# Overflow loads on GpSimd's queue, the next layer's rows loaded early, a second gather round moved back, and the last norm's Newton steps on GpSimd, in a two-layer decoder trunk

## The chip, the cores and the metric

The kernel runs on one core of a Trainium2 chip. TensorE (PE in the views; PEld is its weight load) multiplies matrices into PSUM, VectorE (DVE) and ScalarE (ACT) do element-wise work, GpSimd (POOL) a little of it, and SyncE (SP) issues the loads and stores, which 16 DMA engines carry out. An issuing engine works through its instructions in order, so an issue that waits holds all issues behind it on that engine. The metric is device time in microseconds (us).

## The reference

Two layers run on x of 256 tokens by 1024 channels. Each has a token mixer (four branches read one input projection; their outputs are gated, merged and projected) and a mixture of 16 experts in 4 groups, of which every token uses 2 of one group. Behind each sublayer stands a layer norm of 2^0.5 times the input plus the sublayer's output:

```
for l in range(DEPTH):
    mix = token_mixer(x, ...)                                 # w_in, four branches, w_branch, w_o
    x = layer_norm(DEEPNORM_ALPHA * x + mix, ln1_g, ln1_b)
    ffn = hierarchical_moe(x, ...)                            # router, experts of hidden width 256
    x = layer_norm(DEEPNORM_ALPHA * x + ffn, ln2_g, ln2_b)
```

An expert is `silu(x @ w_gate) * (x @ w_up)`, weighted by the router's gate and multiplied with `w_down`. Everything is float32.

## The kernel before, in words

**Weights.** The weights lie in DRAM as units of 128 x 2048 floats, 1 MB each. `Unit` (line 111) loads one with an issue of SP (line 117). A mixer unit is then split: ACT copies it into a rounded high part (line 134), DVE subtracts that from the original into a low part (line 138), and TensorE multiplies high and low parts (`three`, line 229). An expert's three units (gate and up for half of the channels, for the other half, and down) are used unsplit. Their buffers are a ring of 14 (4 of tag `raw`, 10 of tag `sp`, shown as raw and wr); `look(n)` issues units ahead, each as soon as the unit 14 places before it has been used.

**Experts.** The tokens of an expert are gathered by a matmul with a one-hot matrix Q into 64 slots. Two experts make a pair. Six pairs are worked off, with pair numbers 0 to 5, and the last "pair", number 6, holds the four smallest experts with 32 slots each. From expert 6 on, the order is by token count and the unit's address is read from a tile (`unit_of`). `pair(p)` does on TensorE: gate and up of pair p + 1 (`gu`, line 699), transposes (lines 738 and 740), the scatter of pair p - 1 into the four sums `acc` (line 715), the second half of gate and up, and pair p's down projection (`out_`, line 707). ACT and DVE split its result into two parts `yy` (lines 96 and 97). The gathers come in two rounds: the first for pairs 0 to 2, the second in `pair(1)`, eight channel blocks of four matmuls (line 533). Each block goes to one of two PSUM banks of tag `dn` and is evacuated by ACT (line 539) or DVE (line 541), which read gain and bias of the first norm from the rows tile `rw`. The down projection uses the same two banks.

**Overflow.** An expert with more than 64 tokens needs more slots. If the largest one has more, a branch (line 797) issues its three units on SP into `ow` and `od` (`fetch`, line 691), and a second branch (line 852) runs `chunk` with them, interleaved with the last two down projections. A branch in between (line 807, `rare`) holds the loads and the work of further overflowing experts. In the execution shown layer 0 has no overflow, layer 1 has one expert with it, and `rare` is passed over in both.

**Order.** Blocks under `manual()` run on TensorE, ACT and DVE as written; elsewhere, and on SP and GpSimd everywhere, a planner sets the order from its own estimates. Layer l's `rw` and `bc` (gains, biases, small weights) are loaded at the start of `layer` (line 1095), into one buffer each. At the end of a layer's experts come `out6`, `scatter6`, `turn7` and `down7` for the last two pairs, and `ahead(0)` to `ahead(5)`: the splits of the next layer's first three units. The last result is then split (`parts_of` into y7) and scattered, and 14 matmuls without use (`keep_warm`) follow in layer 0.

**Last norm.** `Norm` takes mean and variance, makes a first guess of the inverse root and a halved variance `hv` (line 278), and `newton` improves it three times with two operations of one element per partition (lines 283 and 284). `scale` (line 295) subtracts the mean from the sums in PSUM and multiplies by the gain; `shift` (line 298) multiplies by the root and adds the bias. `norm2` puts the three Newton steps between the scalings.

Of the kernel before, what the change touches and what calls it, by code (L numbers as in the profile page):

```python
# [19 lines left out]
L = 2  # L20
# [49 lines left out]
def trunk(ctx: ExitStack, tc: tile.TileContext, x, xT, wu, rows, brow, lnp, cst, ut, out):  # L70
# [195 lines left out]
    class Norm:  # L266


        def __init__(self, st, mv=None):
            t_ = lambda s_, w=1: sm.tile([P, w], F32, tag="ln" + s_, name=nm("n" + s_))  # L270
            self.mv = mv
            if mv is None:
                self.mv = t_("mv", 2)
                V.bn_aggr(self.mv, st)
            self.v, self.y, self.hv, self.nmu, self.a = t_("v"), t_("y"), t_("hv"), t_("nmu"), t_("a")
            V.tensor_scalar(self.v, self.mv[:, 1:2], EPS, None, op0=OP.add)
            V.tensor_scalar(self.y.bitcast(I32), self.v.bitcast(I32), -0.5, 1597463007.0, op0=OP.mult, op1=OP.add)
            V.tensor_scalar(self.hv, self.v, -0.5, None, op0=OP.mult)
            if mv is None:
                V.tensor_scalar(self.nmu, self.mv[:, 0:1], -1.0, None, op0=OP.mult)  # L280
# [5 lines left out]
        def all(self):  # L286
            for _ in range(3):
                self.newton()

        def offset(self):  # L290
# [125 lines left out]

    def tail(l, x_in, mhi, mlo, rw, wg, sw, unit, last):

# [117 lines left out]
        def gathered(c, k):  # L536
            g_, b_ = rw[:, W_G1 + k:W_G1 + k + 1], rw[:, W_B1 + k:W_B1 + k + 1]
            if k % 2 == 0:
                A.activation(xg[c][:, k, :], pgs[k], AF.Identity, bias=b_, scale=g_)
            else:  # L540
                V.tensor_scalar(xg[c][:, k, :], pgs[k], g_, b_, op0=OP.mult, op1=OP.add)  # L541

        look(8)
        def keep_warm(q, n, ps):
# [4 lines left out]
        with manual():  # L549
# [88 lines left out]

            def unit_of(i, j):
                eu = nc.values_load(ei[0:1, i:i + 1], engines=(mybir.EngineType.SP,), min_val=l * NU + FIRST_E,  # L640
                                    max_val=l * NU + FIRST_E + 45)
                return wu[bass.ds(eu + j, 1)].rearrange("a p c -> p (a c)")
# [48 lines left out]
            def fetch(i, ww, wd):  # L691
                for j, w in enumerate((ww[:, 0:2048], ww[:, 2048:4096], wd)):
                    nc.sync.dma_start(w, unit_of(i, j))

# [75 lines left out]
            def pair(p, si, todo, ps=None):  # L770
                ps = ps or start(p + 1)
                qt, aT = turn(p, si)
                if todo:
                    scatter(*todo)
                si = end(p + 1, ps)
                for k in more.get(p, ()):
                    for t in range(2):
                        gather(1, k, t)
                    gathered(1, k)
                if p == 1:  # L780
                    slot_gates(STAT // 2, NP)
                return si, out_(p, qt, aT)

# [52 lines left out]
        def scatter6(half):  # L836
            scatter(*todo, (half,), (0,))
# [14 lines left out]
        with tc.If(most > 16 * CAP + 15, label=f"past{l}") as c:  # L852
            with manual():
                steps.chunk(0, CAP, (lambda: out6(0), lambda: out6(1), lambda: scatter6(0),
                                     lambda: (scatter6(1), turn7()), lambda: (ahead(0), down7((0,)))))
                ahead(1)
                down7((1,))
        with c.Else(), manual():
            out6(0)
            out6(1)  # L860
            scatter6(0)
            scatter6(1)
            turn7()
            ahead(0)
            ahead(1)
            down7()
        with manual():
            if last:
                A.activation(gs[:, 0:1], gs[:, 0:1], AF.Square)
            ahead(2)  # L870
            y = mp.tile([P, 2, D], F32, tag="T16a", name=nm("y"))
            y7 = big.tile([P, 2, 2, 512], F32R, tag="xtok", name=nm("y7"))
            yy = [parts_of((ps, tp6)[half], y7[:, half]) for half in range(2)]

            scatter(NP - 1, qt7, yy, (0, 1), (0,))
# [24 lines left out]
            def norm2(t):  # L900
                n_ = Norm(st[t])
                n_.newton()
                for half in range(2):
                    scale(n_, t, half)
                    n_.newton()
                for half in range(2):
                    last_ = shift(n_, t, half)
                return last_
# [3 lines left out]
            if last:  # L912
# [3 lines left out]
                for half in range(2):  # L916
                    A.activation(y[:, 1, HS[half]], acc[1][half], AF.Identity, accum_out=sq[:, half:half + 1])
                n0 = Norm(st[0])
                n0.newton()
                scale(n0, 0, 0)  # L920
                n0.newton()
# [5 lines left out]
                n0.newton()  # L927
                shift(n0, 0, 0)
# [3 lines left out]
                V.tensor_scalar(mv[:, 1:2], sq[:, 2:3], sq[:, 3:4], 1.0 / D, op0=OP.add, op1=OP.mult)  # L932
                n1 = Norm(None, mv)
                n1.newton()
                scale(n1, 1, 0)
                n1.newton()
                scale(n1, 1, 1)
                n1.newton()
                for half in range(2):
                    shift(n1, 1, half)  # L940
                    done(1, half)
            else:
# [11 lines left out]
                nc.sync.dma_start(x2d, y)  # L954
        return None if last else (x2d, nhi, nlo, us[len(feed):])

# [117 lines left out]

    def layer(l, x_in, thi, tlo, last, early):

# [14 lines left out]
        us = [unit() for _ in range(2)]  # L1091
        rw = big.tile([P, W_N], F32, tag="rw", name=nm("rw"))
        bc = big.tile([P, B_N], F32, tag="bc", name=nm("bc"))
        with tc.issue_after(early[2].load.ins) if l == 0 else nullcontext():
            nc.sync.dma_start(rw, rows[l])
            nc.sync.dma_start(bc, brow[l].partition_broadcast(P))

# [265 lines left out]

        return tail(l, x_in, mhi, mlo, rw, wg, sw, unit, last)

    xt, (thi, tlo) = x, first
    for l in range(L):
        r = layer(l, xt, thi, tlo, l == L - 1, early)
        if r is not None:
            xt, thi, tlo, early = r  # L1370

# [110 lines left out]
```

## Time and profile before

| | |
|---|---|
| median of 3 runs | 689.94 us (687.84 to 691.34) |
| profiled execution | 687.56 us, span 685.8 us, mean granted clock 0.986 |
| PE busy | 652.8 us (95%) |
| PEld busy | 462.3 us (67%) |
| DVE busy | 412.3 us (60%) |
| ACT busy | 287.0 us (42%) |
| POOL busy | 5.9 us (1%), 26 instructions |
| DMA | 185.73 MB, mean 271 GB/s, all on one queue |
| raw and wr units from SP | 91 and 63 of 1024 KB, landing 5.2 and 9.5 us (median) after the issue |
| rows (rw) and brow (bc) | 2 of 478 KB and 2 of 458 KB |

The span is the time on the core; some 1.7 us of the device time lie around it. Busy shares are means over stages: in the experts the DMA engines are at times fully busy, in the mixers they are not. The chain of work that ended last goes back only to 647.87 us, so what set the time earlier is read from the timelines and the waits.

### The profile page before, as it was taken

How to read it: one execution, taken by the hardware profiler on the slowest of the kernel's cores; microseconds unless marked ns; L12 is line 12 of the kernel's file. 1: busy time of each engine (PE TensorE's matmuls, PEld its weight loads, DVE VectorE, ACT ScalarE, POOL GpSimd, SP SyncE). 2: the span in 40 equal slices, each digit the busy share in tenths (PEclk: the TensorE clock that was granted, in tenths of full speed). 3: DMA queues.
4: the chain of work that ended last, by engine and by line, in shares of the span. 5: the costliest groups of instructions: out<-in, count | busy, mean ns of one | idle time of the engine just before them, and what ended most of it. 6: DMA issues, size and time to landing. Idle time of an engine off the chain costs nothing. (4 is left out here: it accounts for less than half of the span.)

```text
span 685.8 us, 9776 instructions
## 1 busy us (share of the span) xinstructions
PE 652.8 (95%) x3579; PEld 462.3 (67%) x3579; DVE 412.3 (60%) x932; ACT 287.0 (42%) x465; POOL 5.9 (1%) x26
## 2 busy tenths in 40 slices
PE   8999999999999999998699999999999999999983
PEld 5899778888888354333479987888887953543331
DVE  4998667876557832211799875786853677321116
ACT  5755675454224231111455547664441252211122
POOL 0100000000000000000000000000000000000000
PEclk9999999999999999999899999999999999999997
DMA  8995544466759997979927363456566799699871
GB/s 302 369 338 190 206 131 176 172 219 224 289 192 391 410 419 290 396 291 424 421 100 275 123 236 105 152 183 249 182 225 265 271 409 421 261 402 418 318 326 62
DMA packets 28001, 185.73 MB, mean 271 GB/s; under 512 B 3104, under 2 KB 3232, under 8 KB 6432
## 3 DMA queue, kind: packets, MB, share of 16 engines
q1 hardware_dynamic: 27936, 184.94, 70.4%
q8 instruction: 32, 0.52, 0.3%
q14 instruction: 33, 0.27, 0.1%
HBM read 182.83 MB, written 2.10 MB: 270 GB/s over the span
## 5 line engine op out<-in xcount | busy, mean ns | idle before, releaser
L138 DVE TENSOR_TENSOR sp<-raw,sp 128x1024 fp32r<-128x1024 f32 x122 | 147.9, 1221 | 53.7 <-ACT sp L134 43.6
L134 ACT CAST sp<-raw 128x1024 fp32r<-128x1024 f32 x122 | 126.0, 1051 | 105.3 <-PE mm L229 72.5
L229 PE MATMUL mm<-sp,thi 128*128 128x512 f32 (+1 forms) x320 | 96.5, 382 | 1.5 <-ACT sp L96 0.9
L229 PE MATMUL mm<-sp,nhi 128*128 128x512 f32 (+1 forms) x320 | 97.4, 382 | 0.3 <-ACT nhi L96 0.3
L699 PE MATMUL ps<-wr,xg 128*64 128x512 f32 (+1 forms) x352 | 80.0, 596 | 0.0
L229 PEld LDWEIGHTS mm<-sp,thi 128*128 128x128 f32 x320 | 58.9, 188 | 13.5 <-ACT sp L96 1.5
L229 PEld LDWEIGHTS mm<-sp,nhi 128*128 128x128 f32 x320 | 58.8, 188 | 11.7 <-issue 0.5
L229 PE MATMUL mm<-sp,nlo 128*128 128x512 f32 (+1 forms) x160 | 61.4, 385 | 0.5 <-DVE nlo L97 0.4
L229 PE MATMUL mm<-sp,tlo 128*128 128x512 f32 (+1 forms) x160 | 60.1, 380 | 0.0
L699 PEld LDWEIGHTS ps<-wr,xg 128*64 128x64 f32 (+1 forms) x352 | 23.0, 128 | 37.2 <-issue 36.5
L229 PE MATMUL dn<-sp,yhl 128*128 128x512 f32 x192 | 47.8, 392 | 0.0
L409 DVE SCALAR_TENSOR_TENSOR si<-ps,gs,si 128x256 f32<-128x256 f32 x14 | 6.8, 483 | 62.6 <-ACT si L408 62.4
L699 PE MATMUL ps<-raw,xg 128*64 128x512 f32 (+1 forms) x144 | 43.2, 596 | 0.8 <-DVE xg L541 0.8
L229 PE MATMUL mm<-sp,mhl 128*128 128x512 f32 (+1 forms) x192 | 41.0, 368 | 0.9 <-ACT mhl L96 0.5
L229 PEld LDWEIGHTS dn<-sp,yhl 128*128 128x128 f32 x192 | 35.8, 188 | 7.4
L229 PEld LDWEIGHTS mm<-sp,mhl 128*128 128x128 f32 x192 | 32.6, 189 | 7.5 <-DVE mhl L97 1.1
L229 PE MATMUL mm<-thi,sp 128*128 128x256 f32 x192 | 35.6, 286 | 1.4 <-ACT scr L1225 1.3
L229 PE MATMUL mm<-nhi,sp 128*128 128x256 f32 x192 | 35.7, 286 | 0.3 <-ACT misc L1122 0.3
L97 DVE TENSOR_TENSOR yy<-dn,yy 128x512 fp32r<-128x512 f32 x24 | 16.4, 690 | 31.8 <-ACT yy L96 31.8
L229 PEld LDWEIGHTS mm<-sp,nlo 128*128 128x128 f32 x160 | 30.1, 188 | 6.6 <-DVE nlo L97 1.0
L229 PEld LDWEIGHTS mm<-sp,tlo 128*128 128x128 f32 x160 | 30.1, 188 | 5.5
L707 PE MATMUL dn<-wr,aT 128*64 128x512 f32 x112 | 31.5, 613 | 2.2 <-DMA wr<-in_wu_dram 2.2
(305 smaller groups left out, 974.8 us busy)
## 6 DMA issues: line engine op xcount, KB each, us to landing
raw<-in_wu_dram SPq DMA_DIRECT2D x91, 1024.0 KB, 5.2
wr<-in_wu_dram SPq DMA_DIRECT2D x63, 1024.0 KB, 9.5
w<-in_wu_dram SPq DMA_DIRECT2D x6, 1024.0 KB, 14.9
raw<-in_wu_dram SPq DMA_DIRECT2D x8, 256.0 KB, 6.0
lnp<-in_lnp_dram SPq DMA_DIRECT2D x4, 512.0 KB, 6.0
lnp<-in_lnp_dram SPq DMA_DIRECT2D x2, 1024.0 KB, 15.7
ow<-in_wu_dram SPq DMA_DIRECT2D x2, 1024.0 KB, 10.6
xr<-in_xT_dram SPq DMA_DIRECT2D x4, 256.0 KB, 5.8
```

The costliest lines, as they stand in the source:

```text
L97: eng.tensor_tensor(lo, src, f32(hi), op=OP.subtract)
L134: A.copy(self.parts[q][0], self.raw[:, q * 1024:(q + 1) * 1024])
L138: V.tensor_tensor(lo, self.raw[:, q * 1024:(q + 1) * 1024], f32(hi), op=OP.subtract)
L229: T.matmul(ps, a, b, start=(first and i == 0), stop=(last and i == n - 1))
L409: V.scalar_tensor_tensor(si, ps[:, 256:512], gate, si, op0=OP.mult, op1=OP.mult)
L699: T.matmul(ps[r, :], x_[:, 4 * kh + k, c], w_[:, k * 512:(k + 1) * 512], start=(kh == 0 and k == 0), stop=(kh == 1 and k == 3))
L707: T.matmul(pd[half][r, :], aT[:, k, r], w_[:, k * 1024 + half * 512:k * 1024 + (half + 1) * 512], start=(k == 0), stop=(k == 1))
```

## The change

- `fetch` issues its three loads on GpSimd's queue instead of SP's, in the branch at line 797 and in `rare`; the addresses are read on GpSimd.
- Gains and biases of the first norm (16 columns of `rw`) are copied into a tile `gb` of their own at the start of a layer, and the gathers' evacuations read that. Rows and brow of the next layer are issued in the tail of this one, between the sixth and the seventh expert unit.
- In `pair`, the down projection stands ahead of the second gather round.
- `down7` runs in one piece in the overflow's branch, ahead of its last scatter, and the last split (`parts_of` into y7) stands ahead of `ahead(1)` and `ahead(2)`.
- In the second norm all Newton steps run on GpSimd, as six `tensor_scalar` operations, beside the scalings; the negated mean is no longer made there.

```diff
+        def aside(self):
+            for _ in range(3):
+                G.tensor_scalar(self.a, self.y, self.hv[:, 0:1], self.y[:, 0:1], op0=OP.mult, op1=OP.mult)
+                G.tensor_scalar(self.y, self.a, 1.5, self.y[:, 0:1], op0=OP.add, op1=OP.mult)
...
+    def load_rows(l):
+        rw = big.tile([P, W_N], F32, tag="rw", name=nm("rw"))
+        bc = big.tile([P, B_N], F32, tag="bc", name=nm("bc"))
+        nc.sync.dma_start(rw, rows[l])
+        nc.sync.dma_start(bc, brow[l].partition_broadcast(P))
+        return rw, bc
...
-            g_, b_ = rw[:, W_G1 + k:W_G1 + k + 1], rw[:, W_B1 + k:W_B1 + k + 1]
+            g_, b_ = gb[:, k:k + 1], gb[:, KD + k:KD + k + 1]
...
+        look(6)
+        nxt = None if last else load_rows(l + 1)
         look(8)
...
-                    nc.sync.dma_start(w, unit_of(i, j))
+                    G.dma_start(w, unit_of(i, j, mybir.EngineType.Pool))
...
                 si = end(p + 1, ps)
+                todo = out_(p, qt, aT)
                 for k in more.get(p, ()):
                     for t in range(2):
                         gather(1, k, t)
                     gathered(1, k)
                 if p == 1:
                     slot_gates(STAT // 2, NP)
-                return si, out_(p, qt, aT)
+                return si, todo
...
-                                     lambda: (scatter6(1), turn7()), lambda: (ahead(0), down7((0,)))))
-                ahead(1)
-                down7((1,))
+                                     lambda: (scatter6(1), turn7()), lambda: (ahead(0), down7())))
...
             ahead(0)
-            ahead(1)
             down7()
...
-            ahead(2)
             y = mp.tile([P, 2, D], F32, tag="T16a", name=nm("y"))
             y7 = big.tile([P, 2, 2, 512], F32R, tag="xtok", name=nm("y7"))
             yy = [parts_of((ps, tp6)[half], y7[:, half]) for half in range(2)]
+            ahead(1)
+            ahead(2)
...
             def norm2(t):
-                n_ = Norm(st[t])
-                n_.newton()
+                n_ = Norm(st[t], offset=False)
+                n_.aside()
                 for half in range(2):
                     scale(n_, t, half)
-                    n_.newton()
...
+        gb = sm.tile([P, 2 * KD], F32, tag="gb", name=nm("gb"))
+        V.tensor_copy(gb, rw[:, W_G1:W_G1 + 2 * KD])
```

The norms of the last layer's end are changed in the same way as `norm2`.

## Rows read from the trace of the kernel before

**Rows 1.** The page's first part: busy us (share of span), instructions.
```profile
PE 652.8 (95%) x3579; PEld 462.3 (67%) x3579; DVE 412.3 (60%) x932; ACT 287.0 (42%) x465; POOL 5.9 (1%) x26
```

**Rows 2.** Stretches: length, busy by engine (instructions), granted clock, DMA share, GB/s.
```profile
257.50:265.00 7.50, 7.50 (x40) 3.27 (x40) 3.95 (x12) 1.71 (x3) 0.64 (x1) 1.00 0.45 120
302.50:310.00 7.50, 7.50 (x52) 3.43 (x48) 1.06 (x2) 1.24 (x3) 0.00 (x0) 1.00 0.37 142
592.50:600.00 7.50, 7.50 (x40) 3.37 (x40) 3.14 (x9) 1.80 (x3) 0.00 (x0) 1.00 0.25 62
645.00:650.00 5.00, 5.00 (x52) 1.67 (x51) 0.48 (x1) 0.43 (x2) 0.00 (x0) 1.00 0.38 93
329.40:336.20 6.80, 3.76 (x8) 2.70 (x9) 6.10 (x11) 4.26 (x6) 0.00 (x0) 0.50 1.02 423
```

**Rows 3.** What SP waited for, whole run: total us, times, longest us.
```profile
SPq L807 <- SPq L807: 31.2, 10, 5.6
...
SPq L117 <- PE dn L707: 23.7, 7, 11.8
...
SPq L1095 <- DVE xg L541: 8.2, 1, 8.2
```

**Rows 4.** Line 807 on SP, layers 0 and 1: durations ns, first and last start.
```profile
L807 SPq EVENT_SEMAPHORE  x9: 17/17/17, 299.3 to 306.4; - x9
...
L807 SPq EVENT_SEMAPHORE  x9: 17/17/17, 633.9 to 647.8; - x9
```

**Rows 5.** TensorE's timeline: start us, us, what, count [idle before, releaser].
```profile
322.77 0.62 PE L707 MATMUL ps<-raw,aT 128*32 128x512 f32 x1 [1.34 <-DMA raw<-in_wu_dram]
...
331.86 0.79 PE L715 MATMUL mm<-y,QT 128*128 128x512 f32 x1 [5.47 <-ACT y L96]
...
653.08 3.18 PE L707 MATMUL dn<-wr,aT 128*64 128x512 f32 x6 [2.19 <-DMA wr<-in_wu_dram]
...
658.60 1.94 PE L707 MATMUL dn<-wr,aT 128*64 128x512 f32 x8
```

**Rows 6.** ACT's timeline at the end of layer 0.
```profile
327.76 1.99 ACT L134 CAST sp<-raw 128x1024 fp32r<-128x1024 f32 x2 [7.17 <-issue]
330.28 1.04 ACT L134 CAST sp<-wr 128x1024 fp32r<-128x1024 f32 x1 [0.52 <-DMA wr<-in_wu_dram]
331.23 1.07 ACT L96 CAST y<-ps 128x512 fp32r<-128x512 f32 x2
```

**Rows 7.** DVE's timeline at the end of layer 0.
```profile
328.84 2.36 DVE L138 TENSOR_TENSOR sp<-raw,sp 128x1024 fp32r<-128x1024 f32 x2 [9.92 <-DMA wr<-in_wu_dram]
...
332.50 1.28 DVE L97 TENSOR_TENSOR y<-ps,y 128x512 fp32r<-128x512 f32 x2
...
338.75 1.41 DVE L298 SCALAR_TENSOR_TENSOR y<-y,ny,lnp 128x512 f32<-128x512 f32 x2
```

**Rows 8.** GpSimd's timeline: a memset, a cast, a select.
```profile
0.32 0.10 POOL L1471 MEMSET const-float32-0.0<- 128x1 f32 x1 [0.32 <-issue]
...
17.68 1.17 POOL L198 CAST identb<-cs 128x128 bf16<-128x128 f32 x1 [15.93 <-DMA cs<-in_cst_dram]
...
20.12 0.63 POOL L1164 TENSOR_SCALAR_AFFINE_SELECT rw<-rw 128x512 f32<-128x512 f32 x1
```

**Rows 9.** DVE's timeline beside these casts.
```profile
17.47 2.46 DVE L138 TENSOR_TENSOR sp<-raw,sp 128x1024 fp32r<-128x1024 f32 x2 [2.24 <-ACT sp L134]
```

**Rows 10.** DVE's timeline at the end of layer 1.
```profile
671.31 0.69 DVE L97 TENSOR_TENSOR y<-ps,y 128x512 fp32r<-128x512 f32 x1 [1.19 <-ACT y L96]
...
678.56 0.14 DVE L278 TENSOR_SCALAR nhv<-nv 128x1 f32<-128x1 f32 x1
...
679.07 0.74 DVE L295 SCALAR_TENSOR_TENSOR y<-mm,sq,lnp 128x512 f32<-128x512 f32 x1
...
681.16 1.41 DVE L298 SCALAR_TENSOR_TENSOR y<-y,ny,lnp 128x512 f32<-128x512 f32 x2
```

**Rows 11.** Line 533 in layer 0's second round: durations ns, first and last start.
```profile
L533 PE MATMUL dn<-Q,xh x16: 389/396/500, 249.8 to 257.6; 128*128 128x512 f32 x16
```

More of the change, by code (lines that the diff above doesn't have):

```diff
@@ L266, in trunk, with __init__ @@
     class Norm:
-        def __init__(self, st, mv=None):
+        def __init__(self, st, mv=None, offset=True):
             t_ = lambda s_, w=1: sm.tile([P, w], F32, tag="ln" + s_, name=nm("n" + s_))
@@ L278, in __init__ @@
             V.tensor_scalar(self.hv, self.v, -0.5, None, op0=OP.mult)
-            if mv is None:
+            if offset:
                 V.tensor_scalar(self.nmu, self.mv[:, 0:1], -1.0, None, op0=OP.mult)
@@ L415, in parts_of, with tail @@
         return yy
-    def tail(l, x_in, mhi, mlo, rw, wg, sw, unit, last):
+    def load_rows(l):
[4 more added lines that the diff above has]
+        return rw, bc
+    def tail(l, x_in, mhi, mlo, gb, wg, sw, unit, last):
         tks = [slice(0, P), slice(P, 2 * P)]
@@ L637, in counts, with unit_of @@
                 V.tensor_scalar(ei, ei, -3, 45 + l * NU + FIRST_E, op0=OP.mult, op1=OP.add)
-            def unit_of(i, j):
-                eu = nc.values_load(ei[0:1, i:i + 1], engines=(mybir.EngineType.SP,), min_val=l * NU + FIRST_E,
+            def unit_of(i, j, engine=mybir.EngineType.SP):
+                eu = nc.values_load(ei[0:1, i:i + 1], engines=(engine,), min_val=l * NU + FIRST_E,
                                     max_val=l * NU + FIRST_E + 45)
@@ L917, in tail @@
                     A.activation(y[:, 1, HS[half]], acc[1][half], AF.Identity, accum_out=sq[:, half:half + 1])
-                n0 = Norm(st[0])
-                n0.newton()
+                n0 = Norm(st[0], offset=False)
+                n0.aside()
                 scale(n0, 0, 0)
-                n0.newton()
                 scale(n0, 0, 1)
@@ L926, in tail @@
                     A.activation(y[:, 1, HS[half]], acc[1][half], AF.Square, bias=nmu, accum_out=sq[:, 2 + half:3 + half])
-                n0.newton()
                 shift(n0, 0, 0)
@@ L932, in tail @@
                 V.tensor_scalar(mv[:, 1:2], sq[:, 2:3], sq[:, 3:4], 1.0 / D, op0=OP.add, op1=OP.mult)
-                n1 = Norm(None, mv)
-                n1.newton()
+                n1 = Norm(None, mv, offset=False)
+                n1.aside()
                 scale(n1, 1, 0)
-                n1.newton()
                 scale(n1, 1, 1)
-                n1.newton()
                 for half in range(2):
@@ L954, in tail @@
                 nc.sync.dma_start(x2d, y)
-        return None if last else (x2d, nhi, nlo, us[len(feed):])
+        return None if last else (x2d, nhi, nlo, us[len(feed):], nxt)
     def overflow(topi, counts, spare, fetch, ww, wd, oo, q, gt, x1, sums):
@@ L1073, in overflow, with layer @@
         return SimpleNamespace(chunk=chunk, rare=rare, room=room)
-    def layer(l, x_in, thi, tlo, last, early):
+    def layer(l, x_in, thi, tlo, last, early, rwbc):
         nxt_u = [0]
@@ L1091, in layer @@
         us = [unit() for _ in range(2)]
[L1092 to L1096, printed above, removed]
+        if l == 0:
+            with tc.issue_after(early[2].load.ins):
+                rwbc = load_rows(0)
+        rw, bc = rwbc
+        gb = sm.tile([P, 2 * KD], F32, tag="gb", name=nm("gb"))
+        V.tensor_copy(gb, rw[:, W_G1:W_G1 + 2 * KD])
         misc = big.tile([P, 2048], F32, tag="xtok", name=nm("misc"))
@@ L1362, in layer @@
                 split(tp.rearrange("p (k c) -> p k c", k=4), mhi[d], mlo[d])
-        return tail(l, x_in, mhi, mlo, rw, wg, sw, unit, last)
-    xt, (thi, tlo) = x, first
+        return tail(l, x_in, mhi, mlo, gb, wg, sw, unit, last)
+    xt, (thi, tlo), rwbc = x, first, None
     for l in range(L):
-        r = layer(l, xt, thi, tlo, l == L - 1, early)
+        r = layer(l, xt, thi, tlo, l == L - 1, early, rwbc)
         if r is not None:
-            xt, thi, tlo, early = r
+            xt, thi, tlo, early, rwbc = r
 def constants():
```

## The prediction

> **What bounds the kernel now.** I read the page's busy line first. TensorE is busy 652.8 of 685.8 us and GpSimd 5.9 us in 26 instructions [rows 1]: little is to be won unless TensorE's gaps close, and GpSimd has room. Next, TensorE's timeline at the two places where it stands still for long. At the end of layer 0's experts it waits 1.34 us for a weight and then 5.47 us for ACT's copy of the last expert result, so it idles from 326.39 to 331.86. At the last experts of layer 1 it waits 2.19 us for a weight, and the six matmuls behind take 3.18 us where eight take 1.94 [rows 5]. Third, the table of stretches. After the first idle time the granted clock is 0.50 (1.2 GHz, the lower level) over 6.8 us. The same table shows the DMA engines standing still in four earlier stretches although weights are wanted later: of 7.5, 7.5, 7.5 and 5 us they are busy 0.45, 0.37, 0.25 and 0.38. That is 4.1, 4.7, 5.6 and 3.1 us without transfer, while TensorE is fully busy [rows 2]. Fourth, what SP waited for. The first stretch: 8.2 us at line 1095, the load of the next layer's rows, held until line 541 has read the old rows. The third: 11.8 us (the longest of its seven) until pair 1's down projection (line 707) frees a buffer [rows 3]. The second and fourth lie under SP's stay at line 807, the branch of the rare overflow: nine waits from 299.3 to 306.4 and from 633.9 to 647.8 [rows 4]. 1 MB at 423 GB/s [rows 2] is 2.5 us; nine waits over 13.9 us fit loads landing one after the other. I read them as SP emptying its queue because the branch holds loads of SP. So the late weights come from SP's order, not from too little bandwidth.
>
> **The change part by part.**
>
> *Overflow fetch on GpSimd.* With no load of SP in that branch, the nine waits go, and SP issues the next weights as buffers come free. Each fetch takes its offsets and three issues to GpSimd; behind it stand a few memsets and the last norm, far later. The 3 MB are the same 7.4 us at 423 GB/s on whichever queue. They would start when their buffers are free, in the stretch 592.5 to 600 that has 5.6 us to spare [rows 2], and are read only after 658.60 [rows 5]. No row shows a load issued by GpSimd; up to the 58 us between 600 and 658 it costs nothing, beyond that its excess. I take nothing.
> By the Trainium skill (DMA: Bandwidth & Descriptors, "Issuing engines are not separate DMA queues") a second issuing engine saves only issue time. By that rule this edit gains nothing by itself; the rows of line 807 show a cost that is order and not bandwidth. It is the third case below.
>
> *Rows early.* The copy of 16 columns into gb frees the rows' buffer early, so the load needs no line 541, and SP's 8.2 us go. rows and brow (0.94 MB, 2.2 us) leave this stretch for the token mixer. The copy is one small DVE operation per layer, like those of 0.14 us [rows 10], in a stretch where DVE is not the bound: nothing.
>
> *Second round reordered.* Pair 1's down projection goes ahead of the eight gathers, which run from 249.8 to about 258 [rows 11]. Its weight buffers are free some 8 us earlier, so SP's 11.8 us shrink to about 3. The price is in PSUM: the gathers use the same two banks as the down projection. The second bank is free after a copy and a subtraction of a half (0.54 and 0.69 us from the last parts [rows 6, 10], with handing over 1.4 us), the first gather lasts 1.0 us, and the second waits about 0.5 us. With two layers +1.0 us; bounds 0 and +2.8 (both halves uncovered).
>
> *Layer 0's end.* Before, ACT does two weight copies (327.76, 1.99 us), waits for a further weight (330.28) and only then copies the result (331.23) [rows 6]. Now one copy stands ahead. 4.1 + 4.7 us of DMA standstill are filled, so the first weight is there about 319 to 320, not 327.76, and is copied before the matmuls end. TensorE loses its 1.34 us wait and ends at 325.05. The second half is copied at 325.1 to 325.65 and subtracted to 326.4. What is late next: DVE now has two weight subtractions (2.36 us) ahead of the statistics. Before, from the end of the last subtraction (332.50 + 1.28 = 333.78) to the first shift (338.75) went 4.97 us [rows 7]. Now the shift starts at 326.4 + 2.36 + 4.97 = 333.7, less 0.3 for the norm below: 333.4. With the low clock gone from the scatter it may be 0.4 us less. I take 333.2: -5.5 us. Bounds: -1.8 (weights land no earlier: the copy at 328.8, the shift near 337) and -7.9 (the two subtractions cost nothing).
>
> *Layer 1's last experts.* The weight that TensorE waits for until 653.08 lands 5.3 us after SP's last wait at line 807 (647.8), two loads' time [rows 4, 5]. With that stay gone, or with the 5.6 us of the third stretch filled, it lands before TensorE asks. The wait goes, -2.19; the six matmuls behind it, at the pace of the eight, take 1.94 x 6/8 = 1.46 instead of 3.18, -1.72 [rows 5]. Together -3.9 us; at the other end nothing.
>
> *Both halves ahead of the overflow's scatter, layer 1.* The first half's split hides beside the second half's matmuls, and the second's beside the overflow's scatter; before, DVE ended the last split at 671.31 + 0.69 = 672.0 and the statistics stood behind it [rows 10]. I take -0.7, bounds 0 and -1.3.
>
> *Newton steps on GpSimd.* Three pairs on DVE interleaved with two scalings: from the line that halves v (678.56) to the shift (681.16) 2.60 us, of which the two scalings (0.74 each) are 1.4 [rows 10]. Now six dependent operations on GpSimd run beside the scalings. No row shows such an operation. Ends: a memset of one element 0.10 us, a cast of 128 elements 1.17 us; nearest, because it reads and writes, is the affine select, 0.63 us for 512 elements [rows 8]. One element should cost clearly less, so I take 0.35: 2.1 us and 0.1 for handing over, -0.3 us for each norm on the path. Two in layer 1 (-0.6), one counted above, layer 0's second beside TensorE's work. Ends: 0.10 leaves the scalings as the bound, -1.2 each; 1.17 makes 7.1 us, +4.5 each.
> The Trainium skill (GPSIMD Engine Reference, "Performance pitfalls for Q7 kernels") gives about 102 cycles for each small read command, not overlapped. With three reads an operation at its 1.2 GHz that is an estimate of 1.5 us for six, and the sum below would be 2 us lower; no row shows it.
>
> **The sum:** -5.5 - 3.9 - 0.7 - 0.6 + 1.0 = -9.7 us. The profiled execution took 687.56 us (span 685.8 and 1.7 around it), so 677.9. It is the fastest of those shown; the median is 689.94, and on that scale the forecast is 680.2. I say 680.
>
> **The rivals.**
> 1. *GpSimd's Newton steps become the bound (slower).* At 1.17 us an operation, 7.1 us a norm: layer 0's first norm +4.5, its second holds DVE ahead of the next layer's weight splits (as much again, taken as +4), the two last +4.5 each. 17.5 - 9.7 with the 0.9 taken back: +8.7, 698.6. It decides from 5 us a norm, 0.8 us an operation. For it: the two casts at 1.17 us, the only plain element-wise GpSimd operations that read. Against: a select of four times the size takes half as long [rows 8], and beside the casts DVE ran two subtractions with both inputs in SBUF, 2.46 us in all, and each cast lasted as long as one of them [rows 9]: they look held up, and the scalings here read PSUM.
> 2. *Weights land no earlier (no change).* The freed buffers, not SP's waits, set the issues, or a wait of the same kind reappears elsewhere. Then layer 0 keeps -1.8, the last experts nothing, the tail and norms -1.3, the banks +1.0: -2.1, 687.8. Against: layer 1's late weight was there two loads' time after the end of line 807 [rows 4, 5], so its buffer had been free before.
> 3. *The branch still empties SP's queue; the other edits work.* The queue is emptied 4.1 us earlier in layer 0 and 5.6 us in layer 1. Next layer's first weight lands at 323.7 and is copied by 324.7: still in time; layer 1's late weight lands near 647.5, also in time. Only about 1 us is lost: 681.
> 4. *Only one of the two boundaries closes* (a scheduler-made order elsewhere or a bank stall takes the other): -4 to -6, 685.
>
> **How the numbers follow.** Forecast 0.68 with its own range 674 to 684 (GpSimd cheap -2, the two subtractions free -2, a planner's order outside the hand-ordered blocks +-2); rival 3 0.07, rival 4 0.08, rival 2 0.08, rival 1 0.09. No change is within 0.5% (3.4 us), about what a measurement can tell. Faster: the forecast, rivals 3 and 4, 0.83; same: rival 2 and the near part of rival 1, 0.09; slower 0.08. The range 673 to 687.8 holds all but rival 1, about 0.85 with what the bounds add outside.
>
> **What would show it.** Right: no nine waits at SP's line 807 and no 8.2 us at the rows' load; DMA share near 1.0 where it was 0.25 to 0.45; no granted clock of 0.50 at either place; the last expert copies of layer 0 begin within 1 us of their matmuls; TensorE's wait in layer 1's last down projection gone. Right for the price: a second gather waiting about 0.5 us for its bank. Wrong: GpSimd operations of 0.8 us or more between the halving and the shift, DVE idle there over 2 us; an ACT wait for a weight ahead of the last copy; or the drained queue seen again at another line.

## The result, and the profile after

The changed kernel takes 680.43 us (median of 4 runs, 679.28 to 682.28); the kernel before, run beside it, 688.89 us (686.89 to 691.34). The ratio is 0.9878, 95% interval 0.9836 to 0.992. The forecast was 680. The profiled execution took 680.74 us, its span 679.1, 6.7 us less than before.

Its busy line, to be read against [rows 1]: TensorE does the same 3579 matmuls in 1 us less, GpSimd has 27 instructions more.

```profile
PE 651.8 (96%) x3579; PEld 464.1 (68%) x3579; DVE 408.7 (60%) x907; ACT 289.5 (43%) x467; POOL 15.3 (2%) x53
```

To see where the 6.7 us are, I took the start of the same matmul in both TensorE timelines, at eight places. The table gives how much time each stretch lost (+) or gained (-) against the kernel before, for the changed kernel and for all experiments below. Places are times of the kernel before: 25 is behind the first weights, 205 the end of layer 0's mixer, 221 the first gate and up matmul, 318 to 356 the end of layer 0's experts, 656 the end of the first half of layer 1's down projection for pair 5 [rows 5], 671 the last scatter. "End" is what lies behind 671, "total" the difference of the spans.

```
             to 25  25-205  205-221  221-318  318-356  356-600  600-656  656-671   end   total
changed      +0.27   +1.14    +2.82    +0.52    -6.33    +0.50    -4.50    -0.65  -0.47   -6.7
E1           +0.27   +1.15    +1.26    +0.48    -3.50    +0.44    -1.56    -0.69  +0.95   -1.2
E2           -0.11   -0.01    +0.02    +0.02    -3.75    +0.00    -4.50    +0.01  -0.17   -8.5
E3           -0.16   +1.14    +0.04    +0.41    -6.86    +0.51    -4.46    -0.65  -0.47  -10.5
E4           +0.80   +1.14    +1.26    +0.42    -6.85    +0.45    -4.50    -0.66  -0.47   -8.4
E5           -0.26   -0.01    -0.01    -0.01    -1.46    +0.06    -1.58    -0.67  +0.05   -3.9
E6           +0.16   -0.01    +0.02    -0.04    -5.25    +0.04    -4.49    -0.65  -0.16  -10.4
E7           +0.11   +1.16    +0.00    -0.01    -5.49    +0.03    -4.50    -0.68  -0.43   -9.8
E8           +1.38   +1.13    +0.02    +0.54    -6.52    +0.48    -4.51    +0.99  -0.21   -6.7
E9           -0.07   +1.15    +1.28    -0.02    -5.60    +0.03    -4.52    -0.66  -0.19   -8.6
E10          -0.18   -0.02    +0.02    +0.02    -5.50    -0.01    -4.50    -0.65  -0.19  -11.0
E11          +0.25   -0.01    -0.00    +0.01    -6.26    +0.02    -0.88    -0.65  -0.17   -7.7
E12          +1.50   -0.01    +0.02    +0.01    -5.81    +0.03    -4.50    +0.96  -0.21   -8.0
```

The first column is chance: how the first loads fall out differs by 1.8 us between executions. So is a half clock (the granted clock at the lower of its two levels, 1.2 GHz) in 656-671: +0.99 and +0.96 in E8 and E12, whose code there is that of kernels without it. The other columns repeat to about 0.1 us between kernels with the same code and clock in that stretch, finer than the timed intervals. (E1's +0.95 at the end lies behind the last issue of the output's stores, where no edit stands: from there to the end of the span it has 4.1 us, the changed kernel 2.7.)

**The gains** are where they were expected. Line 807 is now 823. Its waits left SP (18 before, nine in each layer [rows 4]) and went to GpSimd's queue, where nothing stands behind them for a long time:

```profile
L823 POOLq EVENT_SEMAPHORE  x10: 17/42/43, 300.4 to 630.0; - x10
...
L823 SPq EVENT_SEMAPHORE  x2: 17/17/17, 294.7 to 624.0; - x2
```

The DMA engines are full at the four times that [rows 2] show idle; for the first of them this is only half of the story (below). These rows are the table of stretches: length, busy by engine, granted clock, DMA share, GB/s. The last row is the one place at the end of layer 0 where the clock is still at its lower level; the row before it answers to the 0.50 of [rows 2].

```profile
258.00:265.00 7.00, 6.69 (x27) 4.46 (x26) 2.85 (x4) 2.56 (x4) 0.00 (x0) 1.00 1.00 415
303.00:310.00 7.00, 7.00 (x40) 2.47 (x40) 1.87 (x3) 1.56 (x3) 0.00 (x0) 1.00 1.03 420
597.00:604.00 7.00, 7.00 (x36) 3.22 (x34) 0.65 (x5) 0.65 (x2) 0.00 (x0) 1.00 1.02 418
645.00:650.00 5.00, 5.00 (x50) 1.66 (x44) 0.48 (x1) 0.76 (x2) 0.00 (x0) 1.00 1.02 423
...
329.40:336.20 6.80, 6.11 (x25) 4.43 (x24) 6.15 (x11) 4.18 (x6) 1.09 (x4) 1.00 1.01 420
...
340.10:343.50 3.40, 3.12 (x7) 2.48 (x8) 3.30 (x10) 3.38 (x4) 0.49 (x2) 0.51 0.36 147
```

Layer 0's first standstill did not go, it moved. TensorE's work of 257.5 to 265 comes 4.1 to 4.7 us later here, and the idle stretch comes later too. SP's wait for pair 1's down projection (now line 722) fell from 11.8 to 2.3 us, and in each layer a wait of 12.0 us for gate and up matmuls (line 714) took its place, ending at 270.9 and 600.3 us. In layer 1 the DMA engines stay busy through it, because the overflow's loads, now GpSimd's, run at that time. The stretch behind the first row above, and what SP waited for over the whole run:

```profile
265.00:272.00 7.00, 7.00 (x37) 3.80 (x36) 2.01 (x8) 1.25 (x3) 0.00 (x0) 1.00 0.28 90
```

```profile
SPq L117 <- PE ps L714: 69.4, 16, 12.0
...
SPq L117 <- PE dn L722: 18.4, 8, 2.3
```

At the end of layer 0 one weight copy is done before the last matmuls end, and the copies of the result wait for TensorE, not for a weight [rows 6]. ACT's timeline:

```profile
325.69 1.04 ACT L134 CAST sp<-raw 128x1024 fp32r<-128x1024 f32 x1 [0.34 <-DMA raw<-in_wu_dram]
327.12 0.59 ACT L96 CAST y<-ps 128x512 fp32r<-128x512 f32 x1 [0.38 <-PE ps L722]
328.89 0.59 ACT L96 CAST y<-ps 128x512 fp32r<-128x512 f32 x1 [1.18 <-PE ps L722]
```

In layer 1 TensorE's wait of 2.19 us is gone and all eight matmuls run at full pace [rows 5]:

```profile
648.74 1.94 PE L722 MATMUL dn<-wr,aT 128*64 128x512 f32 x8
```

**The losses** were not expected: 1.14 us in layer 0's mixer and 2.82 between it and the experts. The rows of layer 1 are the cause (line 426 is SP's issue of `rw`). In the code the load stands among the expert units; the planner issued it at 59.1 us, in layer 0's mixer, 200 us earlier than before. From 74.6 us on TensorE's matmuls in the mixer come in another order than before. And the three DVE operations on layer 1's router weights (1137, 1138, 1140) were put into the middle of layer 0's router chain. SP's issues, DVE and TensorE:

```profile
L426 SPq DMA_DIRECT2D rw<-in_rows_dram x2: 327/328/328, 10.7 to 59.1; - x2
```

```profile
215.97 0.33 DVE L1137 TENSOR_TENSOR wg<-rw 128x160 f32<-128x160 f32 x1 [0.28 <-PE dn L517]
216.22 0.32 DVE L1138 TENSOR_TENSOR wg<-rw 128x160 f32<-128x160 f32 x1
...
216.58 0.77 DVE L1140 TENSOR_REDUCE wsum<-wg 128x40 f32<-128x320 f32 x1
...
218.89 0.18 DVE L337 SCALAR_TENSOR_TENSOR rsel<-rrk,rgs 128x16 bf16<-128x16 f32 x1
```

```profile
219.12 0.17 PE L618 MATMUL ps<-rsel,oneb 128*128 128x16 bf16 x1 [1.68 <-DVE rsel L337]
```

TensorE waits 1.68 us for the selection of the second token half, at a place where the kernel before waited 0.41:

```profile
216.44 0.17 PE L603 MATMUL ps<-rsel,oneb 128*128 128x16 bf16 x1 [0.41 <-DVE rsel L331]
```

Then the clock was at its lower level from 220.6 us for 3.4 us and took another 1.55 us; E1, E4 and E9, with the same wait, had no such stretch, so the wait alone does not bring those 1.55 us.

**The norms** on GpSimd run as long as on DVE. GpSimd's timeline of the last norm, and DVE's halving ahead and shift behind it: 672.02 to 674.63 is 2.61 us, before 2.60 [rows 10]. An operation lasts 0.27 to 0.35 us but starts only 0.36 to 0.45 after the one before.

```profile
672.26 0.34 POOL L293 TENSOR_SCALAR na<-ny,nhv 128x1 f32<-128x1 f32 x1 [2.11 <-DVE nhv L278]
672.71 0.27 POOL L294 TENSOR_SCALAR ny<-na,ny 128x1 f32<-128x1 f32 x1
673.07 0.34 POOL L293 TENSOR_SCALAR na<-ny,nhv 128x1 f32<-128x1 f32 x1
...
674.33 0.27 POOL L294 TENSOR_SCALAR ny<-na,ny 128x1 f32<-128x1 f32 x1
```

```profile
672.02 0.14 DVE L278 TENSOR_SCALAR nhv<-nv 128x1 f32<-128x1 f32 x1
...
674.63 1.41 DVE L304 SCALAR_TENSOR_TENSOR y<-y,ny,lnp 128x512 f32<-128x512 f32 x2 [1.15 <-POOL ny L294]
```

### The profile page after: what moved, and what is told of

Its sections match the earlier page's. It is cut to its first block, busy times and chain, and to the rows that moved or that the text cites. A ratio compares the mean times of both kernels' runs of the same rounds, so it can differ in the third digit from the quotient of the medians.

```text
span 679.1 us, 9792 instructions
## 1 busy us (share of the span) xinstructions
PE 651.8 (96%) x3579; PEld 464.1 (68%) x3579; DVE 408.7 (60%) x907; ACT 289.5 (43%) x467; POOL 15.3 (2%) x53
## 5 line engine op out<-in xcount | busy, mean ns | idle before, releaser
L229 PEld LDWEIGHTS mm<-thi,sp 128*128 128x128 f32 x192 | 30.1, 191 | 2.0 <-ACT scr L1235 1.5
```

The costliest lines, as they stand in the source:

```text
L229: T.matmul(ps, a, b, start=(first and i == 0), stop=(last and i == n - 1))
```

## The experiments

The theory after the traces: the empty-queue wait of SP at the rare branch made the weights late, and moving the fetch alone removes it; the early rows give part of it back. The rivals: all the order edits are needed together, or the buffers set the issues and the branch is beside the point.

**E1 and E2: the fetch alone, undone and done.** E1 is the changed kernel with

```diff
-                    G.dma_start(w, unit_of(i, j, mybir.EngineType.Pool))
+                    nc.sync.dma_start(w, unit_of(i, j))
```

> The changed kernel (680.4 us) with the overflow's three loads back on SP's queue. Theory A (a branch that holds loads of SP makes SP empty its queue): the nine waits come back at the rare branch in both layers, DMA share falls below 0.5 in the stretches around 300 to 310 and 640 to 650 us, and since rows and second round stay early the weights keep most of their lead: about +1 us, 681.4. Theory B (the lead came from the fetch alone): the late weights come back too, PE waits about 2 us in layer 1's last down projection and the clock halves behind it, +4 to +6 us, 684 to 686. Theory C (the waits had another cause): no nine waits, no change, 680.4.

Measured: 687.3 us, ratio to the kernel before 0.9992 (0.9976 to 1.0007). Without this line all the other edits together bring nothing that the times can tell. SP has its 18 waits back, and the late weight too. The DMA engines, full near 260 and 590 us, stand still later instead:

```profile
L823 SPq EVENT_SEMAPHORE  x18: 17/17/17, 302.1 to 647.6; - x18
```

```profile
303.00:310.00 7.00, 7.00 (x44) 2.34 (x44) 1.87 (x3) 1.56 (x3) 0.00 (x0) 1.00 0.45 151
597.00:604.00 7.00, 7.00 (x39) 3.81 (x39) 1.73 (x7) 0.65 (x2) 0.00 (x0) 1.00 0.31 88
645.00:650.00 5.00, 5.00 (x52) 1.67 (x51) 0.39 (x1) 0.39 (x1) 0.00 (x0) 1.00 0.33 72
```

```profile
652.86 1.93 PE L722 MATMUL dn<-wr,aT 128*64 128x512 f32 x6 [1.87 <-DMA wr<-in_wu_dram]
```

That is theory B's mechanism, and 1.3 us above its range, though the clock did not fall behind TensorE's wait in this execution; the +1 us of theory A (the third rival) was far too small. What the early rows and the second round bring forward near 260 and 595 us is lost again, at 265 to 270 (a DMA share of 0.05) and 597 to 604 before the branch is reached, and then while the queue is emptied.

E2 is the kernel before with the same line changed the other way (and the address read on GpSimd).

> The kernel before (688.9 us) with this edit alone: the overflow's loads on GpSimd's queue. Theory A (SP's emptied queue made both weights late): the nine waits go; layer 1's last down projection loses its wait of 2.19 us and the half-clock matmuls, -3.9; at the end of layer 0 the weights land about 4 us earlier but ACT still copies weights first, -2 to -3; together -6 to -7, 682 to 683. Theory B (buffers, not the queue, set the issues): under -1 us, 688 to 689, with DMA share as low as before in the stretches near 260 and 595 us and the late weights late as before.

Measured: 679.25 us, 0.9871 (0.9845 to 0.9896), 2.7 us below the range of theory A. The row of 257.5 to 265 still shows a DMA share of 0.46; the row behind the branch, 0.37 before, is 1.01. TensorE no longer waits for a weight, but at the end of layer 0 ACT waits for two that it copies ahead of the result, and TensorE waits 2.85 us for ACT.

```profile
257.50:265.00 7.50, 7.50 (x39) 3.22 (x39) 3.84 (x12) 1.61 (x3) 0.64 (x1) 1.00 0.46 122
302.50:310.00 7.50, 7.50 (x52) 3.43 (x48) 0.98 (x2) 1.24 (x3) 0.00 (x0) 1.00 1.01 417
592.50:600.00 7.50, 7.50 (x38) 3.41 (x36) 1.39 (x2) 1.69 (x4) 0.00 (x0) 1.00 1.01 418
```

```profile
322.74 1.99 ACT L134 CAST sp<-raw 128x1024 fp32r<-128x1024 f32 x2 [2.23 <-DMA raw<-in_wu_dram]
325.20 1.04 ACT L134 CAST sp<-wr 128x1024 fp32r<-128x1024 f32 x1 [0.47 <-DMA wr<-in_wu_dram]
```

```profile
326.78 0.61 PE L715 MATMUL mm<-y,QT 128*128 128x512 f32 x1 [2.85 <-ACT y L96]
```

Layer 0 has no overflow, so its 3.75 us come from the waits alone. In layer 1 the edit does two things at once: the waits go, and the overflow's three loads, which SP issued at 612 to 614 us, are issued by GpSimd at 582 to 590 and fill the third stretch of [rows 2] (0.25 before, 1.01 here). No run separates the two, so which of them makes layer 1's -4.50 is not shown.

**E3: the router's weights held back.**

```diff
-        V.tensor_tensor(wg[:, :, 0:20], wr, rw[:, W_G1:W_G1 + 8, None]...)
+        with tc.issue_after(behind[0].ins) if l else nullcontext():   # behind[0]: residual split
+            V.tensor_tensor(wg[:, :, 0:20], wr, rw[:, W_G1:W_G1 + 8, None]...)
...
```

> The changed kernel with the next layer's three DVE operations on the router's weights (wg, wg, wsum) held behind the first residual split of the experts; nothing else is reordered. Theory A (they stand in layer 0's router chain on DVE and cost PE 1.27 us of waiting, after which the clock halves for 3.4 us and costs 1.2 more): PE's wait for the second token half's selection falls from 1.68 to about 0.4 us, no granted clock of 0.50 near 220 us, -2.5 us, 678.0. Theory B (the clock falls for another reason): the wait falls, the clock drop stays, -1.3 us, 679.2. Theory C (PE waits for something else next): within 0.3 us of 680.4.

Measured: 678.23 us, 0.986 (0.9834 to 0.9887). The wait is 0.41 us again and the stretch 205-221 costs +0.04 instead of +1.26 (+2.82 with the half clock). The intervals of E3 and the changed kernel overlap, so the times alone do not show it; the table and the wait do. Theory A holds for the wait. The clock fell behind the long wait in one of the four executions that have it, and behind none of the short ones.

**E4: more filler matmuls.**

```diff
-                keep_warm(Q[0], 14, psumd())
+                keep_warm(Q[0], 22, psumd())
```

> The changed kernel with 22 instead of 14 filler matmuls at the end of layer 0, 1.9 us more. Theory A (PE's idle 2.24 us ahead of the transposes makes the clock halve at 340 us): the idle time shrinks to about 0.3 us, the clock stays at 1.0 there, -1.5 us, 678.9. Theory B (the clock falls for the thin work behind the idle time, or the fillers hold up the transposes): 0 to +0.5 us, 680.4 to 680.9, with the 0.50 stretch still there.

Measured: 679.31 us, 0.9873 (0.985 to 0.9896), not to be told from the changed kernel. The idle time fell from 2.24 to 0.42 us and the clock stayed at 1.0, as theory A has it, but the stretch gains 0.5 us (-6.85 for -6.33), not 1.5: E3, with 14 fillers and 1.91 us idle, kept its clock as well and shows the same -6.86.

**E5 and E6: the last expert's edit, without and with the fetch.**

```diff
             ahead(0)
-            ahead(1)
             down7()
...
-            ahead(2)
             y = mp.tile([P, 2, D], F32, tag="T16a", name=nm("y"))
             yy = [parts_of((ps, tp6)[half], y7[:, half]) for half in range(2)]
+            ahead(1)
+            ahead(2)
```

and `down7()` in one piece in the overflow's branch. E5 is the kernel before with this edit.

> The kernel before (688.1 us beside it) with the last expert's edit alone: its copies and subtractions stand ahead of the weight splits of the second and third step, and the last down projection runs in one piece ahead of the overflow's scatter. The weights stay late. Theory A (this edit works only with early weights): one weight copy still waits for its load ahead of the expert result, so the end of layer 0 gains 1 to 2 us (one copy of 1.0 us and the wait of 0.5 us less), layer 1's tail 0.7; about -2, 686. Theory B (the order of ACT, not the load, made the wait): the boundary closes, -5 or more, 683. Theory C: no change, 688.

Measured: 685.36 us, 0.9966 (0.9947 to 0.9985); 1.46 us at the end of layer 0, 0.67 in layer 1's tail: theory A. (The 1.58 us at 600-656 are a half clock that did not come; the wait of 1.85 us is there.)

E6 adds the fetch of E2.

> The kernel before with two edits: the overflow's loads on GpSimd's queue (alone it took 679.25 us) and the last expert's edit. Theory A (the two add up): PE's wait of 2.85 us for ACT's copy at the end of layer 0 goes and the clock stays at 1.0 there, -2; layer 1's tail -0.7; together 676.5, which is below the changed kernel (680.4), because the rows loaded early, the second round and the norms on GpSimd, which are left out, cost more than they bring. Theory B (the early rows are needed for the weights to be early enough): the first weight is copied later than the last matmuls end and the wait stays; 678.5 to 679.5.

Measured: 676.0 us (675.83 to 677.0), 0.9821 (0.9807 to 0.9835), the fastest of all. The two edits add up: 3.75 + 1.46 = 5.21 at the end of layer 0, measured 5.25. Theory A, with one reserve: the next layer's first weight is somewhat late for ACT, and TensorE waits 1.13 us:

```profile
325.27 0.50 PE L715 MATMUL mm<-y,QT 128*128 128x512 f32 x1 [1.13 <-ACT y L96]
```

**E7: the second round put back** (on E3: the gathers again ahead of pair 1's down projection).

```diff
-                todo = out_(p, qt, aT)
                 for k in more.get(p, ()):
...
-                return si, todo
+                return si, out_(p, qt, aT)
```

> The changed kernel with the router's weights held (678.2 us) and the second gather round back ahead of pair 1's down projection. Theory A (the bank waits are its price, and nothing needs the earlier buffers any more): the gathers' waits of 0.3 us each go, -0.7 us in two layers, 677.5; SP's longest wait for pair 1's down projection is 11 to 12 us again and the DMA share near 257 to 265 us falls to about 0.5 without a late weight. Theory B (the earlier buffers carry the weights of the end): a wait for a weight comes back at the end of layer 0 or in layer 1, +1.5 to +4, 680 to 682.

Measured: 677.87 us, 0.985 (0.9832 to 0.9869); E3 has 678.23. The price goes (0.41 and 0.51 us to nothing in the stretches 221-318 and 356-600), and a price at the end of layer 0 comes: -5.49 for -6.86, with a half clock again. Neither theory alone: the edit pays 0.9 us and gets 1.4 back, some 0.5 of it the half clock (the changed kernel beside E3); the times do not tell the two kernels apart.

**E8: the Newton steps back on DVE** (on E3: `newton()` between the scalings in place of `aside()`).

> The changed kernel with the router's weights held (678.2 us) and the last norms' Newton steps back on DVE between the scalings. Theory A (six operations on GpSimd take 2.4 us beside 1.4 us of scalings, as long as the interleaved chain of 2.6 us): within 0.3 us, 678.0 to 678.5. Theory B (as the prediction had it, 0.3 us for each of three norms on the path): +0.9, 679.1. Theory C (GpSimd is late: the steps on DVE are shorter): -0.6 or more, 677.6 or less.

Measured: 678.94 us, 0.9859 (0.9841 to 0.9878): theory A. From the halving to the shift the trace has 2.59, 2.90 and 2.59 us for the three norms on the path; with GpSimd 2.60 each. Only the middle one gains, because two DVE operations of the next statistics stand in its chain. The column "end" agrees: -0.47 with GpSimd, -0.2 without.

**E9: the early rows added to E6** (the copy `gb`, the loads in the tail, nothing held; that is the changed kernel with E7's and E8's edits).

> The kernel of two edits (fetch on GpSimd, last expert's edit; 676.0 us) with the early rows added: the copy of gain and bias, the loads in the tail, nothing held. Theory A (the early rows let the next layer's row work into layer 0's mixer and router chain): the experts of layer 0 begin 3 to 4 us later (the first gate and up matmul near 225 us, not 221.4), PE waits 1.7 us for the second half's selection; the weight at the end of layer 0 comes early enough that PE's wait of 1.1 us for ACT goes; in all +2 to +3, 678 to 679. Theory B (the second round moved back made the loss): 676 or less. Theory C (it is a chance order of the planner in the changed kernel alone): the start near 221.4 and 675.5.

Measured: 679.43 us, 0.9878 (0.9852 to 0.9905): theory A. It loses 1.15 us in the mixer and 1.28 in the router, and gains 0.35 at the end of layer 0. The other half of theory A fails, and the loss is 3.4 us by the medians, above its 2 to 3: TensorE's wait of 1.1 us for ACT at the end of layer 0 is still there (1.12). It is gone in the changed kernel, E3, E4 and E8, which have the second round moved as well.

```profile
218.78 0.17 PE L618 MATMUL ps<-rsel,oneb 128*128 128x16 bf16 x1 [1.67 <-DVE rsel L337]
```

**E10: 21 fillers on E6** (`keep_warm(Q[0], 21, psumd())`).

> The kernel of two edits (676.0 us) with 21 instead of 14 filler matmuls at the end of layer 0, 1.7 us more of PE's idle 1.88 us. Theory A: the idle time falls to about 0.2 us, no granted clock of 0.50 behind it (there it cost 1.5 us), 674.5. Theory B (another idle time makes the clock fall, or the fillers come in the way): the 0.50 stretch stays, 675.8 to 676.5.

Measured: 677.12 us, 0.9843 (0.9819 to 0.9868), no gain over E6 (0.9821). The lower level of the clock is gone, the stretch gains only 0.25 us. Beside E10, E6's matmuls lost 1.3 us from 337 to 340 us and had 0.9 of them back by 350, at places where TensorE waits for DVE and ACT in E10 too.

**E11: a use for DVE's idle time beside GpSimd.** On E6: layer 0's two norms on GpSimd, and one weight subtraction of each (`ahead(2)`, `ahead(4)`) moved between scalings and shift; 16 fillers.

```diff
+                n_.aside()
                 for half in range(2):
                     scale(n_, t, half)
-                    n_.newton()
+                ahead(6 + t)                      # one ("low", i, 0) each
```

> The kernel of two edits (676.0 us) with the Newton steps of layer 0's two last norms on GpSimd, and in DVE's idle 1.15 us between scalings and shift one weight subtraction each that stood ahead of the statistics or behind the shift; 16 filler matmuls, since PE's idle time shrinks. Theory A (the time on GpSimd is free for DVE to use): the statistics of the first norm begin 1.1 to 1.2 us earlier, from the halving to the shift it stays at 2.6 to 2.7 us, no clock of 0.50 behind it; -1.1 -1.5, 673.4. Theory B (a DVE subtraction with both inputs in SBUF holds GpSimd up): the GpSimd operations beside it take over 1 us, the shift is late by about 1.2 us and the gain is gone, 674.5 to 675.5.

Measured: 680.6 us, 0.989 (0.9866 to 0.9913). That is above both theories. Theory B's mechanism is there: the GpSimd operation that meets DVE's subtraction lasts 1.27 us instead of 0.27, and from halving (329.72) to shift it is 3.62 us instead of 2.60. GpSimd, then DVE:

```profile
330.41 0.27 POOL L289 TENSOR_SCALAR ny<-na,ny 128x1 f32<-128x1 f32 x1
...
331.23 1.27 POOL L289 TENSOR_SCALAR ny<-na,ny 128x1 f32<-128x1 f32 x1
```

```profile
331.15 1.22 DVE L138 TENSOR_TENSOR sp<-wr,sp 128x1024 fp32r<-128x1024 f32 x1
333.34 1.41 DVE L303 SCALAR_TENSOR_TENSOR y<-y,ny,lnp 128x512 f32<-128x512 f32 x2 [0.97 <-POOL ny L289]
```

The end of layer 0 still comes out at -6.26, 1.0 us better than E6, so theory B's loss does not show there. What makes the kernel slow is elsewhere: at the rare branch of layer 1 TensorE waits 2.32 us for its own sequencer (0.30 to 0.37 in the other kernels), and the clock halves behind it, together 3.6 us (-0.88 for -4.49).

```profile
625.27 2.97 PE L720 MATMUL mm<-yy,QT 128*128 128x512 f32 x8 [2.32 <-PEq L812]
```

Nothing was edited there. Why this branch is slow in this kernel I leave open.

**E12: the early rows tied down** (on E6: the load of `rw` behind the sixth expert unit's load, the copy `gb` and the router's weights behind the residual splits).

```diff
+        with tc.issue_after(behind_.ins) if behind_ else nullcontext():   # us[5].load
+            nc.sync.dma_start(rw, rows[l])
...
```

> The kernel of two edits (676.0 us) with the early rows, but tied down: the next layer's rows are issued behind the sixth expert unit's load, where the text of the changed kernel has them (its SP order has them 28th of all issues, in layer 0's mixer), and the copy of gain and bias and the router's weights stand behind the experts' residual splits. Theory A (the loss came from the place to which the planner moved the rows and the work on them): the first gate and up matmul of layer 0 begins near 221.5 us, not 225.6; the weight at the end of layer 0 is early, so PE's wait of 1.1 us for ACT goes; 675.0 to 675.5. Theory B (layer 0's own copy of gain and bias already changes the mixer's order): it begins near 222.5 to 223 us, 676.5. Theory C (early rows cost by their mere traffic): near 225 us, 679.

Measured: 676.94 us, 0.9836 (0.9809 to 0.9862). `rw` is now issued at 186.3 us, and the mixer and the router lose nothing (-0.01, +0.02): theory A on the cause, and layer 0's own copy is free. E3, where only the router's weights are held, keeps the mixer's loss, so that one comes from the load's place or from the copy `gb` for layer 1; which of the two is not separated. On the gain it was wrong: TensorE's wait for ACT falls only from 1.13 to 0.88 us, and the time is that of E6. The early rows are worth nothing here, well placed, and cost 2.4 us as they were placed.

## Why the prediction came out

The time is within half a microsecond of the forecast, and that is partly luck. The forecast was -9.7 us, counted from 689.94; measured are -8.5, counted from 688.89, and the lower start makes up for most of the difference. Within the sum, errors of two kinds cancelled in part.

- **What bounds the kernel: right.** SP's waits at line 807 are the empty queue; they follow the loads to GpSimd's queue, and one edit carries the gain (E2 0.9871, E1 0.9992). In layer 1 the overflow's earlier loads may have a part in it (E2). The Trainium skill's rule that a second issuing engine brings only issue time (DMA: Bandwidth & Descriptors, "Issuing engines are not separate DMA queues") would make this edit worth nothing; E2 disagrees in effect, not in kind: no byte moves faster, but the waits no longer hold SP.
- **All four stretches of idle DMA counted alike and taken as filled: wrong.** The first was not filled, it moved behind 265 us (0.28), where SP waits 12.0 us for line 714: part of the second rival, a wait of the same kind elsewhere. What it cost is small: next layer's first weight, expected at 319 to 320, landed near 325.6 in the changed kernel, 4.75 us of lost time included, and ACT waited 0.34 us for it. Where it is as before, TensorE waits 1.13 us for ACT (E6). The second, under line 807, cost 3.75 us (E2). In layer 1 the third was filled by the overflow's own loads and the fourth with the end of the waits; their parts in the -4.50 are not separated.
- **Rows and brow, 0.94 MB, leave the first stretch: misread.** Layer 1's brow was issued at 33.0 us already before, so only the rows' half could go.
- **Fetch on GpSimd at 0: right.** Its issues last 0.53 to 0.72 us, and nothing behind them is late.
- **Layer 0's end, -5.5:** -6.3 in the profiled execution, -6.9 where the clock stayed up (E3, E4): it was expected to stay up, and fell at 340.1 us for 3.4 us. E2 and E5 split it into 3.75 for the fetch and 1.46 for the order.
- **Layer 1's last experts, -3.9:** -4.50, in every kernel with the fetch on GpSimd whose rare branch was not slow; 0.5 us more comes from the second of the eight matmuls, which before started 0.5 us behind the first, ahead of the long wait.
- **Both halves ahead of the overflow's scatter, -0.7:** -0.65 (E2, without it, +0.01).
- **Newton on GpSimd, -0.3 a norm:** mis-sized. I took 0.35 us an operation, 2.2 us with handing over (which against 2.60 would be 0.4, not 0.3); it lasts 0.27 to 0.35, but they start 0.4 us apart, so six take 2.4 us and the gain is 0, 0.3 and 0. The estimate worked out from the Trainium skill (GPSIMD Engine Reference, "Performance pitfalls for Q7 kernels"), 1.5 us for six, was lower still; the trace decides, 2.4.
- **Second round, +1.0:** +0.52 and +0.50, as priced. Its gain, part of which I had put into the lead of the weights, is about as large as its price (E7).
- **Rows early at 0: the step that failed.** I wrote that the load leaves for the token mixer and priced the copy `gb` alone. Not priced was what becomes ready with the load: three DVE operations on the next layer's router weights, which a planner without the old wait could put anywhere. It put them into the router's chain (+1.27). The mixer's order changed as well (+1.15), with the load's place or layer 1's copy `gb`. E9 has both losses, E3 takes the first away and E12 both. The trace of before had a hint: `brow`, in the next line of the code, was issued at 33.0 us there, 226 us ahead of `rw`.

So the expected gains measured -6.33 -4.50 -0.65 -0.47 +1.02 = -10.9 against -9.7, and the unpriced +2.4, the chance half clock of 1.55 and 0.27 at the start make the -6.7 of the profiled execution. Without the last two it would be -8.5, the difference of the medians.

Of the rivals, the first did not come: 0.4 us an operation, half of where it decides. The third was priced 6 us too low: with the queue emptied again (E1) the other edits do not make up for it. I had reckoned that the weights keep their lead. E1's DMA share of 0.31 at 597 to 604 us and SP's waits of 12.0 us for line 714 speak for the ring of buffers: a lead ends in a standstill as soon as all buffers are full. No run tried a larger ring.

## What to carry to other kernels

- A wait in front of a branch belongs to the engine whose queue holds the branch's loads, even where the branch isn't taken. Look for it in the waits of the issuing engine, and give rare loads to an engine with nothing behind them.
- A removed wait is also a removed fence: where a planner sets the order, list what becomes ready with it, and tie it down if it shares an engine with a critical chain.
- Edits that come together should be run alone. Here one edit made the gain, one more made it larger by 3 us (E6), and three cost about as much as they brought or more.

## What the runs showed of the hardware

- A GpSimd `tensor_scalar` on 128 x 1, reading its scalars from SBUF, lasts 0.26 to 0.35 us and starts 0.36 to 0.45 us after the one it depends on.
- It lasts 1.27 and 1.29 us beside a DVE subtraction of 1.22 us with both inputs in SBUF (E11), and 0.27 beside scalings that read PSUM. The Trainium skill (SBUF — State Buffer, "SBUF: two separate sides") says that such a DVE operation and a GpSimd one that reads SBUF lock each other out for a whole instruction; the trace agrees.
- The clock's fall is not settled by the idle time ahead of it: at the end of layer 0 it fell behind 1.88 us (E6), 1.91 us (E7) and 2.24 us (changed), and stayed up behind 1.91 us (E3). Where it fell it cost 0.25 us (E6 beside E10) to 0.5 us (changed beside E3) at that place, and 1.55 to 1.65 at the router (changed) and in layer 1's tail (E8, E12).
- The same branch cost TensorE 0.30 to 0.37 us in thirteen kernels and 2.32 us in one (E11, layer 1).
